# Attention weights times values: two fp32 products per query group made as three split products

## The chip, the cores and the metric

The kernel runs on one core of a Trainium2 chip. Its engines work side by side, each through its own queue of instructions in a fixed order: TensorE (PE; its weight loads are listed as PEld), VectorE (DVE), ScalarE (ACT), GpSimd (POOL) and SyncE (SP, which issues most of the DMAs). They wait for one another through semaphores. The metric is the time of one launch on the device, in microseconds; the median of several runs is compared.

## The reference

One layer of a diffusion backbone for two groups of requests: 256 context tokens (`xp`) and 2048 latent tokens (`xs`), model width 1024. What matters here is the differential attention of the latent tokens, 4 heads, keys and values being 512 cached ones and the 2048 latent ones:

```python
def one_block(qblk):
    s = jnp.einsum('bqhmd,bkhmd->bhmqk', qblk, k).astype(jnp.float32) * scale
    p = jax.nn.softmax(s, axis=-1)
    a = p[:, :, 0] - lam * p[:, :, 1]
    return jnp.einsum('bhqk,bkhe->bqhe', a.astype(v.dtype), v)
```

Around it stand a modulated RMS norm and one input projection before, and a Fourier mixing of other channels, an output projection and a squared-ReLU MLP behind. All inputs are float32.

## The kernel before

**Precision.** A float32 product is mostly made as three products of the type `float32r` (`mm3`, lines 85 to 88): each operand is split into a high part (a rounding copy on ScalarE) and a low part (the original minus the high part, on VectorE), and high·high, high·low and low·high are added up in the same PSUM bank. A few products are made directly in float32 instead, with one matmul call and no low part.

**Stages.** Projections of all tokens, Fourier mixing, attention, output projection, MLP. In the projections `v_out` (lines 343 to 351) copies each tile of values out of PSUM; for the latent tokens it stores it to the DRAM scratch `vs`, and `v_split` stores the high and low parts to `vd`.

**Attention of the latent tokens.** For each of 4 heads, 8 groups of 256 queries, two tiles of 128 (`j`). A group has for each `j` two score maps `m` of 128 x 2560. Operations are methods of `Group`:

- `fill` (line 918): two matmuls of 512 keys into one of five PSUM banks `S`
- `rowmax` (L923) and `comb` (L926): row maxima on VectorE and their combination, once for each `(j, m)`
- `exp` (L942): exponentials on ScalarE from the `S` bank to SBUF, `P0` or `P1`; it needs `comb`, and frees the bank
- `combine` (L946 to L965): denominators on VectorE and POOL, then POOL makes P0 + factor·P1, in two pieces
- `tr` (L974): four transposes of a pair of key blocks `kb`, `kb + 1` into one of **two** PSUM banks `pt`
- `ah` (L980): ScalarE copies that bank to SBUF
- `al` (L985): VectorE subtracts the copy from the bank, the low part
- `mul`: six split products per pair (three for each of two key tiles) into `po`, or, for the pairs named in `FULL = (4, 14)`, two fp32 products (L998) with fp32 values `vf4`, `vf14`, loaded by `load_v` (L878). For these pairs the `ah` copy is fp32 and there is no `al`
- `o1` to `o6`: transposing back, RMS sub-norm and store

The ten pairs of a group are 0, 2, ... 18, so two of them, 4 and 14, go by fp32.

**The order of the work is written out by hand.** Each operation is added to a list with a time (`add`), the list is sorted, and each engine gets its instructions in that order (`tc.manual_schedule()`). The unit of the plan is a step `T`, one for each `(j, m)`, divided into 5 `u`; a group has four steps and the next group follows four steps later. In a step a group's five `fill`s stand at 0.76 to 3.4, its `rowmax`es at 1.26 to 3.9, `comb` at 4.55, and the `exp`s at 0 to 2.64 of the step after. In its steps 6 to 9 the group's pairs are transposed: two in steps 6 and 8, three in steps 7 and 9. In a step of three the transposes stand at 0.9, 2.2 and 3.86, the copies at 3.3, 3.8 and 4.4; the fp32 pair is the first of the three. A step's `mul`s stand at 3.9 of the step after. So the `mul`s of a step of two are on TensorE's queue right behind the third transposes of a step of three, and the `mul`s of a step of three, fp32 ones first, at the end of a step of two. `o1` to `o6` fall into every second step of three. The tile framework adds the waits: `tr` takes a bank `pt` only when everything that reads the tile before in it is done. The plan's times set only the order; they are not waited for.

The last group of the last head takes its transposes' banks from the five `S` and the two `pt` in turn (`bank`, `self.edge`), and some of the first two groups' scores do so too. The prompt's own attention (`Prompt`, one for each head) is laid between the groups, and uses the same `pt` banks.

Of the kernel before, what the change touches and what calls it, by code (L numbers as in the profile page):

```python
# [10 lines left out]
F32 = mybir.dt.float32  # L11
F32R = mybir.dt.float32r
# [6 lines left out]
P = 128  # L19
# [3 lines left out]
NS = 2048  # L23
# [5 lines left out]
LAM_INIT = 0.8 - 0.6 * math.exp(-0.3 * 0)  # L29
GRID_W = 64  # L30
TSTEP, AVS = 5.2, 6
FULL = (4, 14)

PSCALE = 512 / math.sqrt(256 * 128)

# [1 line left out]
def f32(ap):  # L37
    return ap.bitcast(F32)


def body(tc, a, out):
    nc = tc.nc
    ctx = ExitStack()
    with ctx:
# [6 lines left out]
        def scratch(name, shape):  # L51
            return dram.tile(shape, F32, tag=name, name=name)

        fp, fs = scratch("fp", [NP, 512]), scratch("fs", [NS // 2, 512])
        fsum, fdif, frev = (scratch(x, [NS // 2, 512]) for x in ("fsum", "fdif", "frev"))
        vs = scratch("vs", [NS, 512])
        NK = (PAST + NS, NP)
        kd = [scratch(f"kd{s}", [H, 2, P, NK[s]]) for s in range(2)]
        vd = [scratch(f"vd{s}", [H, P, NK[s] // P, 2, P]) for s in range(2)]
# [25 lines left out]
        def mm3(ps, lh, ll, rh, rl, first, last):  # L85
            nc.tensor.matmul(ps, lh, rh, start=first, stop=False)  # L86
            nc.tensor.matmul(ps, lh, rl, start=False, stop=False)  # L87
            nc.tensor.matmul(ps, ll, rh, start=False, stop=last)  # L88
# [119 lines left out]
        with ExitStack() as c1:  # L208
# [6 lines left out]
            def t2(nm):  # L215
                return p1.tile([P, 512], F32, tag="t2", name=nm, bufs=6)
# [127 lines left out]
            def v_out(i):  # L344
                s = 1 if i < 2 else 0
                n = i if s else i - 2
                ps = PJ.pop((i, 2))
                o = t2(f"vo{i}")
                nc.scalar.copy(o, ps)
                nc.sync.dma_start(out[3][n * P:n * P + P] if s else vs[n * P:n * P + P], o)  # L350
                return o

            def v_post(i):
# [55 lines left out]
            with tc.manual_schedule():  # L409
# [30 lines left out]
                with tc.tile_pool(name="p0h", bufs=6, reuse_waits="tile") as halves:  # L440
# [51 lines left out]
                    for k in range(KD):  # L492
                        for g in range(4):
                            w = wraw[2 * k + g // 2][:, g % 2 * 512:g % 2 * 512 + 512]
# [149 lines left out]
        with ExitStack() as c2:  # L644
# [106 lines left out]
            with tc.manual_schedule():  # L751
# [30 lines left out]
                A = [None] * 4  # L782
# [58 lines left out]
        with ExitStack() as c3_:  # L841
# [4 lines left out]
            at = c3_.enter_context(tc.tile_pool(name="a_t", bufs=2, reuse_waits="tile"))  # L846
# [5 lines left out]
            class Head:  # L852
# [16 lines left out]
                def load_v(self):  # L869
                    s, h, ak = self.s, self.h, self.ak  # L870
                    self.V = ak.tile([P, self.nkt, 2, P], F32R, tag=f"V_{s}", name=f"V{self.nm}")
                    nc.sync.dma_start(f32(self.V), vd[s][h])
                    self.vf = {}
                    if not s:
                        for kb in FULL:
                            t = ak.tile([P, 2, P], F32, tag=f"vf{kb}", name=f"vf{kb}{self.nm}")
                            r = (kb - 4) * P
                            nc.sync.dma_start(t, vs[r:r + 2 * P, self.hc].rearrange("(t p) e -> p t e", p=P))  # L878
                            self.vf[kb] = t

            class Group:
                def __init__(self, hd, g):
# [92 lines left out]
                    self.pt[kb] = pt  # L975

                def ah(self, kb):
                    full = kb in self.hd.vf
                    t = at.tile([P, 512], F32 if full else F32R, tag="af" if full else "ah", name=f"ah{self.nm}_{kb}", bufs=2 if full else 4)
                    nc.scalar.copy(t, self.pt[kb])  # L980
                    self.A[kb] = [t]

                def al(self, kb):
                    t = at.tile([P, 512], F32R, tag="al", name=f"al{self.nm}_{kb}", bufs=4)
                    nc.vector.tensor_sub(t, self.pt[kb], f32(self.A[kb][0]))  # L985
                    self.A[kb].append(t)

                def mul(self, kb):
                    if self.po is None:
                        self.po = pS.tile([P, 512], F32, tag="po", name=f"po{self.nm}")  # L990
                    A = self.A.pop(kb)
                    for t in range(2):
                        c = slice(t * 256, t * 256 + 256)
                        first = self.nmul == 0
                        self.nmul += 1
                        last = self.nmul == self.hd.nkt
                        if len(A) == 1:
                            nc.tensor.matmul(self.po[:, 0:256], self.hd.vf[kb][:, t, :], A[0][:, c], start=first, stop=last)  # L998
                        else:
                            mm3(self.po[:, 0:256], self.hd.V[:, kb + t, 0, :], self.hd.V[:, kb + t, 1, :], A[0][:, c], A[1][:, c], first, last)  # L1000

                def o1(self):
                    self.oT = at.tile([P, 256], F32, tag="oT", name=f"oT{self.nm}")
# [81 lines left out]
            def add(t, fn, *args):  # L1085
                ev.append((t, len(ev), fn, args))

            T = TSTEP
            u = T / 5.0
# [11 lines left out]
            for h in range(H):  # L1101
                hd, hp = Head(0, h), Head(1, h)
                base = h * 32 * T
                add(base - 18 * T + 0.7 if h else -3.04 * T, hd.load_k)
                add(base - 14 * T + 0.7 if h else 0.9 * T, hd.load_v)
                add(base - 13 * T + 0.7 if h else 0.91 * T, hp.load_k)
                add(base - 13 * T + 0.71 if h else 0.92 * T, hp.load_v)
                gp, r = Prompt(hp, 0), base + 10 * T
                add(r - 2 * T, gp.qload)
                for j in range(2):  # L1110
                    for t, fn in ((5.25, gp.scores), (5.85, gp.rowmax), (6.33, gp.exp), (8.0, gp.combine)):
                        add(r + t * u, fn, j)
                    r += 2 * T
                for t, fn, *args in ((5.25, gp.tr, 0), (6.33, gp.ah), (6.95, gp.al), (15.25, gp.mul), (16.33, gp.o1),
                                     (25.25, gp.o2), (25.9, gp.o3), (27.32, gp.o4), (28.557, gp.o5), (29.0, gp.o6)):
                    add(r + t * u, fn, *args)
                for g in range(hd.ng):
                    gr = Group(hd, g)
                    add(base - 2 * T + 0.6 * u if base else -3.03 * T, gr.qload)
                    for st in range(4):  # L1120
                        j, m = divmod(st, 2)
                        t0 = base + st * T
                        for b in range(hd.nbk):
                            add(t0 - T + (0.76 + 0.66 * b) * u, gr.fill, j, m, b)
                            add(t0 - T + (1.26 + 0.66 * b) * u, gr.rowmax, j, m, b)
                            add(t0 + 0.66 * b * u, gr.exp, j, m, b)
                        add(t0 - 0.45 * u, gr.comb, j, m)
                        if m:
                            add(t0 + 5.9 * u, gr.combine, j)
                    kbs = list(range(0, hd.nkt, 2))  # L1130
                    for q in range(4):
                        w = base + (AVS + q) * T
                        if q % 2 == 0:
                            order = [kbs.pop(0) for _ in range(2)]
                            tr_t, ah_t, al_t = [0.9, 2.2], [3.3, 3.8], [4.6, 5.2]
                        else:
                            order = [kbs.pop(0) for _ in range(3)]
                            tr_t, ah_t, al_t = [0.9, 2.2, 3.86], [3.3, 3.8, 4.4], [None, 4.6, 5.2]
                        for n, kb in enumerate(order):
                            add(w + tr_t[n] * u, gr.tr, kb)  # L1140
                            add(w + ah_t[n] * u, gr.ah, kb)
                            if al_t[n]:
                                add(w + al_t[n] * u, gr.al, kb)
                            add(w + T + (3.9 + 0.01 * n) * u, gr.mul, kb)
                    w = base + (AVS + 5) * T + 1.0 * u
                    for t, fn in ((0, gr.o1), (0.4, gr.o2), (0.75, gr.o3), (2.32, gr.o4), (3.557, gr.o5), (4.0, gr.o6)):
                        if gr.last and t > 2:
                            LASTO.append(fn)
                        else:
                            add(w + t * u, fn)  # L1150
                    base += 4 * T
# [340 lines left out]
        with c5r, ExitStack() as c5:  # L1492
# [155 lines left out]
            with tc.manual_schedule():  # L1648
                for n, (q, p) in enumerate(ITEMS):
                    b, last = q // NF, q % NF == NF - 1 and q // NF < 2  # L1650
# [71 lines left out]
        with ExitStack() as c6:  # L1722
# [52 lines left out]
            for i in range(7):  # L1775
                for k in range(16):
                    n = i * 16 + k
# [7 lines left out]
            with tc.manual_schedule():  # L1785
                pend, NM, loaded, KS = None, 7 * 24, 4, []
                for i in range(7):
                    for b in range(3):
                        ps = [pp.tile([P, 512], F32, tag="ps", name=f"ps{i}_{b}_{j}", bufs=6) for j in range(3)]
                        for k in range(16):  # L1790
                            n, m = i * 16 + k, (i * 3 + b) * 8 + k // 2
# [18 lines left out]
                            if (i, b) == (6, 2) and 9 <= k < 12:  # L1810

                                j = k - 9
                                u = U3[6 + j]
                                nc.vector.tensor_mul(u, u, g2[0][:, 0:512])
                                nc.vector.tensor_add(u, u, X[j])
                            if i == 0 and b == 1 and k in (2, 6, 10, 14):
                                s, hf = divmod(k // 4, 2)
# [4 lines left out]
                            for j in range(3):  # L1822
                                c = slice(j * P, j * P + P)
# [4 lines left out]
                for j in range(3):  # L1828
                    t = 6 + j
                    c = t6.tile([P, 512], F32, tag="c", name=f"cl{t}", bufs=4)  # L1830
                    nc.vector.tensor_mul(c, ps[j], g2[0][:, 0:512])
                    nc.vector.tensor_sub(c, U3[t], c)
                    r = (t + NTH) * P - NP
# [72 lines left out]
```

## Time and profile before

| | |
|---|---|
| median of 3 runs | 2970.22 us (2969.95 to 2972.25) |
| the profiled execution | 2976.96 us, its span 2975.1 us |
| PE, busy share of the span | 98% |
| DVE | 68% |
| ACT | 53% |
| POOL | 34% |
| mean granted clock of TensorE | 0.993 |

A row of a group reads: line, engine, operation, output tile<-input tiles, shapes, count, then durations. In the timeline a row has start, length, engine, line, operation and, in brackets, how long the engine was idle before it and what ended that. Busy shares overlap: matmuls are pipelined, and a record lasts longer than the time until the next may start. `PEclk` and "granted clock" are the share of its full clock that TensorE was given.

### The profile page before, as it was taken

What the parts mean: (1) busy time and instruction counts of PE and PEld (TensorE: products, weight loads), DVE (VectorE), ACT (ScalarE), POOL (GpSimd) and SP (SyncE); (2) the same over time, 40 slices, a digit from 0 to 9 for tenths busy, and PEclk for the clock granted to TensorE, in tenths of its full rate; (3) what the DMA queues carried; (4) which work ended last, traced back from release to release, by engine and by line L of the source; (5) the groups of instructions that cost most, each with busy time, mean ns of one, the idle gap of its engine ahead of it and who ended that gap; (6) DMA issues with size and microseconds to landing.
All of it is one profiled execution on the core that took longest, in us unless ns stands there. A gap on an engine that the chain in (4) does not pass through costs nothing.

```text
span 2975.1 us, 43755 instructions
## 1 busy us (share of the span) xinstructions
PE 2910.2 (98%) x15417; PEld 2518.0 (85%) x15417; DVE 2016.3 (68%) x3379; ACT 1568.3 (53%) x3540; POOL 1023.9 (34%) x839
## 2 busy tenths in 40 slices
PE   8999999989999999999999999999999999999999
PEld 4888887768888888888889999999999888888887
DVE  6666775678888888875458778777776344344554
ACT  4333322678888888864346556556555322232221
POOL 1111112169898989952222333333332000000000
PEclk9999999989999999999999999999999999999999
DMA  7777878512131211215686677676666454445563
GB/s 274 202 195 198 232 197 250 195 52 84 35 110 37 91 53 34 95 50 157 202 252 213 217 240 225 220 237 214 222 199 229 145 170 163 138 145 173 195 216 107
DMA packets 394414, 495.58 MB, mean 167 GB/s; under 512 B 26403, under 2 KB 307056, under 8 KB 391122
## 3 DMA queue, kind: packets, MB, share of 16 engines
q1 hardware_dynamic: 386560, 477.63, 50.5%
q0 software_dynamic: 2992, 7.28, 0.8%
q10 hardware_dynamic: 4642, 7.88, 0.8%
q8 instruction: 122, 2.00, 0.3%
q14 instruction: 98, 0.80, 0.1%
HBM read 315.20 MB, written 179.57 MB: 166 GB/s over the span
## 4 chain that ended last, share of the span: by engine, by line
PE 84%; ACT 8%; DVE 4%; DMA 2%; issue 1%; POOL 0%; SPq 0%; ACTq 0%; DVEq 0%; POOLq 0%
PE Ss L918 8%; PE ps L86 8%; PE ps L87 8%; PE ps L88 8%; PE pj L86 4%; PE pj L88 4%; PE pj L87 4%; PE pts L974 4%; ACT P1s L942 3%; PE po L88 2%; PE po L86 2%; PE po L87 2%; PE pA L1532 2%; PE pA L1534 2%; PE pA L1533 2%; PE pC L1534 2%
## 5 line engine op out<-in xcount | busy, mean ns | idle before, releaser
L923 DVE TENSOR_REDUCE mxs<-Ss 128x1 f32<-128x512 f32 x640 | 419.4, 687 | 86.8 <-PE Ss L918 77.9
L1227 DVE TENSOR_TENSOR sl<-sr,sh 128x768 fp32r<-128x768 f32 x168 | 161.8, 964 | 339.8 <-ACT sh L1226 339.3
L965 POOL TENSOR_TENSOR P0s<-P0s,P1s 128x1024 f32<-128x1024 f32 x124 | 365.7, 2949 | 10.4
L1226 ACT CAST sh<-sr 128x768 fp32r<-128x768 f32 x168 | 140.2, 835 | 424.9 <-PE ps L87 424.9
L942 ACT ACTIVATE P1s<-Ss,mxs 128x512 f32<-128x512 f32 x320 | 217.2, 694 | 69.3 <-DVE mxs L926 69.3
L1574 POOL TENSOR_TENSOR gs<-g,g 128x384 f32<-128x384 f32 x48 | 70.3, 1464 | 483.7 <-ACT g L1544 376.7
L86 PE MATMUL pj<-wh,hh 128*128 128x512 f32 x576 | 229.8, 399 | 0.7 <-ACT fo L374 0.7
L87 PE MATMUL ps<-tlT,sh 128*128 128x512 f32 x585 | 229.3, 392 | 0.0
L86 PE MATMUL ps<-thT,sh 128*128 128x512 f32 x585 | 229.2, 392 | 0.0
L87 PE MATMUL pj<-wl,hh 128*128 128x512 f32 x576 | 227.7, 395 | 0.7 <-DVE wl L496 0.7
L88 PE MATMUL ps<-thT,sl 128*128 128x512 f32 x585 | 227.7, 389 | 0.0
L88 PE MATMUL pj<-wh,hl 128*128 128x512 f32 x576 | 226.7, 394 | 0.0
L942 ACT ACTIVATE P0s<-Ss,mxs 128x512 f32<-128x512 f32 x320 | 215.8, 696 | 7.8 <-DVE mxs L926 7.7
L918 PE MATMUL Ss<-KS1s,Qs 128*128 128x512 f32 x640 | 199.9, 426 | 13.6 <-ACT P0s L942 11.1
L918 PE MATMUL Ss<-KS0s,Qs 128*128 128x512 f32 x640 | 198.7, 423 | 10.5 <-ACT P1s L942 9.4
L974 PEld LDWEIGHTS pts<-ident,P0s 128*128 128x128 f32 x1280 | 158.0, 141 | 51.7 <-ACT ahs L980 5.7
L974 PE MATMUL pts<-ident,P0s 128*128 128x128 f32 x1280 | 193.0, 274 | 6.3 <-DVE alp L1071 4.1
L1543 ACT ACTIVATE g<-uz 128x384 f32<-128x384 f32 x144 | 75.9, 527 | 207.1 <-DVE uz L1566 180.6
L964 POOL TENSOR_SCALAR P1s<-P1s,tots 128x1024 f32<-128x1024 f32 x124 | 166.7, 1344 | 5.6
L985 DVE TENSOR_TENSOR als<-pts,ahs 128x512 fp32r<-128x512 f32 x256 | 163.9, 681 | 5.3 <-ACT ahs L980 5.3
L86 PE MATMUL ps<-ophT,sh 128*128 128x512 f32 x423 | 165.9, 392 | 1.1 <-DVE uz L1566 1.1
L88 PE MATMUL ps<-ophT,sl 128*128 128x512 f32 x423 | 165.7, 392 | 0.0
(613 smaller groups left out, 8216.1 us busy)
## 6 DMA issues: line engine op xcount, KB each, us to landing
sr<-sd SPq DMA_DIRECT2D x84, 768.0 KB, 4.4
a<-in_w SPq DMA_DIRECT2D x184, 256.0 KB, 3.8
sd<-gs SPq DMA_DIRECT2D x192, 192.0 KB, 1.9
sd<-g SPq DMA_DIRECT2D x144, 192.0 KB, 4.1
wm<-in_w_mod SPq DMA_DIRECT2D x32, 512.0 KB, 5.3
Qs<-qd SPq DMA_DIRECT2D x32, 512.0 KB, 3.7
b<-in_w SPq DMA_DIRECT2D x64, 256.0 KB, 5.2
b<-tsum SPq DMA_DIRECT2D x64, 256.0 KB, 4.6
```

The costliest lines, as they stand in the source:

```text
L86: nc.tensor.matmul(ps, lh, rh, start=first, stop=False)
L87: nc.tensor.matmul(ps, lh, rl, start=False, stop=False)
L88: nc.tensor.matmul(ps, ll, rh, start=False, stop=last)
L918: nc.tensor.matmul(S[:, :w], self.Q[:, x, m, j * P:j * P + P], self.hd.KS[m][:, b * 512:b * 512 + w], start=(x == 0), stop=(x == 1))
L923: nc.vector.tensor_reduce(self.mx[j][:, m, b:b + 1], self.S[j, m, b], axis=AX.X, op=ALU.max)
L942: nc.scalar.activation(dst, S, AF.Exp, bias=self.mx[j][:, m, 6:7], accum_out=self.sm[j][:, m, b:b + 1])
L964: nc.gpsimd.tensor_scalar(p, p, tot[:, 3:4], 0.0, op0=ALU.mult, op1=ALU.add)
L965: nc.gpsimd.tensor_add(d, d, p)
L974: nc.tensor.transpose(pt[:, c:c + P], self.p0[j][:, (kb + t) * P:(kb + t + 1) * P], ident)
L985: nc.vector.tensor_sub(t, self.pt[kb], f32(self.A[kb][0]))
L1226: nc.scalar.copy(hi, src)
L1227: nc.vector.tensor_sub(lo, src, f32(hi))
```

## The change

The two pairs 4 and 14 are treated like the others. Their `ah` copy is `float32r`, they get an `al` subtraction, and `mul` makes six split products of each with the parts of V that are loaded anyway. The fp32 copy of the latent values goes: no scratch `vs`, no stores to it in `v_out`, no `vf` tiles or loads. `ah` and `al` have five buffers each (before four and four, and two for the fp32 copies). In the steps of three the subtractions stand at 4.6, 5.2 and 5.8 of the step (before none, 4.6 and 5.2); transposes and copies keep their places.

```diff
-FULL = (4, 14)
...
-        vs = scratch("vs", [NS, 512])
...
                 nc.scalar.copy(o, ps)
-                nc.sync.dma_start(out[3][n * P:n * P + P] if s else vs[n * P:n * P + P], o)
+                if s:
+                    nc.sync.dma_start(out[3][n * P:n * P + P], o)
                 return o
...
                     nc.sync.dma_start(f32(self.V), vd[s][h])
-                    self.vf = {}
-                    if not s:
-                        for kb in FULL:
-                            t = ak.tile([P, 2, P], F32, tag=f"vf{kb}", name=f"vf{kb}{self.nm}")
-                            r = (kb - 4) * P
-                            nc.sync.dma_start(t, vs[r:r + 2 * P, self.hc].rearrange("(t p) e -> p t e", p=P))
-                            self.vf[kb] = t
...
                 def ah(self, kb):
-                    full = kb in self.hd.vf
-                    t = at.tile([P, 512], F32 if full else F32R, tag="af" if full else "ah", name=f"ah{self.nm}_{kb}", bufs=2 if full else 4)
+                    t = at.tile([P, 512], F32R, tag="ah", name=f"ah{self.nm}_{kb}", bufs=5)
...
                 def al(self, kb):
-                    t = at.tile([P, 512], F32R, tag="al", name=f"al{self.nm}_{kb}", bufs=4)
+                    t = at.tile([P, 512], F32R, tag="al", name=f"al{self.nm}_{kb}", bufs=5)
...
-                        if len(A) == 1:
-                            nc.tensor.matmul(self.po[:, 0:256], self.hd.vf[kb][:, t, :], A[0][:, c], start=first, stop=last)
-                        else:
-                            mm3(self.po[:, 0:256], self.hd.V[:, kb + t, 0, :], self.hd.V[:, kb + t, 1, :], A[0][:, c], A[1][:, c], first, last)
+                        mm3(self.po[:, 0:256], self.hd.V[:, kb + t, 0, :], self.hd.V[:, kb + t, 1, :], A[0][:, c], A[1][:, c], first, last)
...
-                            tr_t, ah_t, al_t = [0.9, 2.2, 3.86], [3.3, 3.8, 4.4], [None, 4.6, 5.2]
+                            tr_t, ah_t, al_t = [0.9, 2.2, 3.86], [3.3, 3.8, 4.4], [4.6, 5.2, 5.8]
                         for n, kb in enumerate(order):
                             add(w + tr_t[n] * u, gr.tr, kb)
                             add(w + ah_t[n] * u, gr.ah, kb)
-                            if al_t[n]:
-                                add(w + al_t[n] * u, gr.al, kb)
+                            add(w + al_t[n] * u, gr.al, kb)
```

## The prediction

> **What bounds the kernel now.** I read the page first, then the windows by stage, then the attention stage's timeline engine by engine.
>
> ```profile
> PE 84%; ACT 8%; DVE 4%; DMA 2%; issue 1%; POOL 0%; SPq 0%; ACTq 0%; DVEq 0%; POOLq 0%
> 150.00:300.00 150.00, 150.00 (x737) 125.06 (x736) 99.47 (x186) 51.16 (x108) 23.87 (x12) 1.00 0.78 200
> 609.00:1326.00 717.00, 698.38 (x4413) 592.95 (x4412) 611.78 (x1199) 618.87 (x1744) 620.58 (x501) 0.99 0.18 63
> L998 PE MATMUL pos<-ahs,vf4s x128: 377/379/382, 624.8 to 1320.1; 128*128 128x256 f32 x128
> L998 PE MATMUL pos<-ahs,vf14s x128: 377/379/382, 635.6 to 1325.0; 128*128 128x256 f32 x128
> L985 DVE TENSOR_TENSOR als<-pts,ahs x256: 675/681/692, 613.5 to 1324.1; 128x512 fp32r<-128x512 f32 x128
> ```
>
> The chain of waits is TensorE's. In the projections (150 to 300 us, where the removed stores are issued) it is never idle. The latent attention with its products fills 609 to 1326 us: 32 groups, 22.4 us each, with PE, DVE, ACT and POOL (the busy columns after the length, PEld second) all between 611 and 698 of 717 us. Four full engines mean that an added wait is not soaked up. Each fp32 product leaves two matmul records (256 records, 128 products, four a group).
>
> A group is four steps; second and fourth ("odd" here) transpose three key-block pairs, the others two. This is one odd step and the even one behind it, on PE.
>
> ```profile
> 902.09 0.62 PE L918 MATMUL Ss<-KS0s,Qs 128*128 128x512 f32 x2
> 904.28 1.17 PE L918 MATMUL Ss<-KS0s,Qs 128*128 128x512 f32 x4
> 905.29 0.60 PE L974 MATMUL pts<-ident,P0s 128*128 128x128 f32 x4
> 905.84 0.28 PE L87 MATMUL pos<-als,Vs 128*128 128x256 f32 x1
> 907.02 0.28 PE L88 MATMUL pos<-ahs,Vs 128*128 128x256 f32 x1
> 907.37 0.73 PE L918 MATMUL Ss<-KS1s,Qs 128*128 128x512 f32 x2
> 910.68 1.02 PE L998 MATMUL pos<-ahs,vf14s 128*128 128x256 f32 x4
> 912.81 0.28 PE L88 MATMUL pos<-ahs,Vs 128*128 128x256 f32 x1
> 912.93 0.63 PE L918 MATMUL Ss<-KS0s,Qs 128*128 128x512 f32 x2
> ```
>
> The odd step takes 907.37 − 902.09 = 5.28 us, the even one 5.56. The third transposes stand at 905.29, and behind them in PE's queue twelve products and the next scores. The other engines then:
>
> ```profile
> 904.46 0.60 ACT L980 COPY ahs<-pts 128x512 f32<-128x512 f32 x1
> 905.12 0.53 PEld L974 LDWEIGHTS pts<-ident,P0s 128*128 128x128 f32 x4
> 905.98 0.59 ACT L980 CAST ahs<-pts 128x512 fp32r<-128x512 f32 x1 [0.43 <-PE pts L974]
> 903.66 2.65 DVE L923 TENSOR_REDUCE mxs<-Ss 128x1 f32<-128x512 f32 x4 [0.21 <-PE Ss L918]
> 906.34 0.16 DVE L926 TENSOR_REDUCE mxs<-mxs 128x1 f32<-128x5 f32 x1
> 906.42 1.28 DVE L985 TENSOR_TENSOR als<-pts,ahs 128x512 fp32r<-128x512 f32 x2
> 908.13 0.69 DVE L923 TENSOR_REDUCE mxs<-Ss 128x1 f32<-128x512 f32 x1 [0.17 <-PE Ss L918]
> 906.53 0.69 ACT L942 ACTIVATE P0s<-Ss,mxs 128x512 f32<-128x512 f32 x1
> 907.37 0.30 PEld L918 LDWEIGHTS Ss<-KS1s,Qs 128*128 128x128 f32 x2 [0.27 <-ACT P0s L942]
> ```
>
> The third transposes load at 905.12, just after the copy of the first pair (904.46 + 0.60) has freed one of the two `pt` banks. That first pair is the fp32 one: copied, never subtracted. DVE's subtractions of the other two begin only at 906.42, behind five row maxima and their combination, and the exponentials' first must follow the third copy (905.98) on ACT; it releases the next step's first scores at 907.37.
>
> **The change part by part.** *Products.* Two fp32 products and twelve split ones take 912.93 − 910.68 = 2.25 us. Ten split intervals from 905.84 to 907.02 are 0.118 us each; eighteen are 2.12. Gain 0.13 us an even step if PE sets its end, nothing if the exponentials do; both lie close, so I take 0.12: 64 × 0.12 = **−8 us** (bounds −8.3 and 0).
>
> *Subtractions.* One more in each odd step, 64 × 0.68 = 44 us of DVE, which has 717 − 612 = 105 us idle in the stage. By itself it is covered by DVE's idle time before the next row maximum; without that cover, see the second rival.
>
> *The new wait.* The first pair is now subtracted too, so its bank is held until that subtraction ends. It is queued on DVE at 4.6 of the step, behind the row maxima and the combination (3.9 and 4.55); the third transposes stay at 3.86 in PE's queue. So PE, which keeps its written order, must wait there. Does such a wait block PE? The trace already has it, once a head, where the prompt's subtraction holds the bank:
>
> ```profile
> 664.91 0.68 DVE L1071 TENSOR_TENSOR alp<-ptp,ahp 128x512 fp32r<-128x512 f32 x1
> 665.71 0.42 PEld L974 LDWEIGHTS pts<-ident,P0s 128*128 128x128 f32 x4 [1.41 <-PE Ss L918]
> PEld pts L974 <- ACT ahs L980: 5.7, 23, 1.9
> PE pts L974 <- DVE alp L1071: 4.1, 4, 1.0
> ```
>
> The transposes load 0.12 us after the subtraction ends (665.59), and nothing behind them passes. So in the step above: first subtraction 906.42 to 907.10, load at 907.22 instead of 905.12, **2.10 us late**. What is late next: transposes, third copy, first exponential (906.53 → 908.63), next scores (907.37 → 909.47), all by 2.10. PE's own twelve products end at 907.14 + 2.10 = 909.24, earlier, so ACT's path sets it. The new third subtraction, at 908.7 behind the third copy, ends before the next row maximum, itself moved to 910.2. The other odd step, four steps of output added:
>
> ```profile
> 915.36 1.17 PE L918 MATMUL Ss<-KS0s,Qs 128*128 128x512 f32 x4
> 916.25 0.48 PEld L974 LDWEIGHTS pts<-ident,P0s 128*128 128x128 f32 x4
> 917.59 1.28 DVE L985 TENSOR_TENSOR als<-pts,ahs 128x512 fp32r<-128x512 f32 x2
> 917.78 0.70 ACT L942 ACTIVATE P0s<-Ss,mxs 128x512 f32<-128x512 f32 x1
> ```
>
> Load at 917.59 + 0.68 + 0.12 = 918.39 instead of 916.25; the third copy then runs 919.2 to 919.8 and the exponential starts 2.02 late. The mean is 2.06. The last group spreads its transposes over seven banks, so 62 of 64 odd steps pay: 62 × 2.06 = **+128 us**. Other odd steps that I read gave 1.83 to 2.18: bounds 113 and 135.
>
> *The clock.* PE's gap in those steps runs from the end of the scores (904.28 + 1.17 = 905.45) to 907.39, and 916.53 to 918.56: about 1.98 us. The trace shows gaps of that kind. Each pair of rows below is a stretch of 3.41 us and the next; after the length stands PE's busy time, third from the end the granted clock.
>
> ```profile
> 574.63:578.04 3.41, 2.04 (x7) 0.89 (x6) 2.93 (x6) 2.68 (x9) 0.00 (x0) 1.00 1.06 354
> 578.04:581.46 3.42, 3.42 (x8) 2.21 (x8) 2.59 (x6) 2.94 (x11) 0.00 (x0) 0.50 0.97 364
> 1298.26:1301.67 3.41, 1.63 (x13) 1.16 (x12) 0.74 (x2) 3.41 (x11) 3.33 (x2) 1.00 0.01 2
> 1301.67:1305.08 3.41, 3.34 (x16) 3.34 (x17) 2.45 (x7) 1.78 (x7) 3.07 (x5) 0.50 0.00 0
> 663.36:666.78 3.42, 2.41 (x16) 1.83 (x14) 2.80 (x5) 3.39 (x13) 3.34 (x2) 1.00 0.00 0
> 666.78:670.19 3.41, 3.34 (x26) 2.87 (x24) 3.17 (x9) 2.63 (x7) 2.01 (x5) 1.00 0.00 0
> 2042.40:2045.80 3.40, 1.99 (x11) 1.83 (x11) 3.16 (x4) 3.37 (x7) 0.00 (x0) 1.00 0.41 130
> 2045.80:2049.20 3.40, 3.40 (x20) 3.18 (x20) 3.40 (x4) 3.01 (x7) 1.35 (x1) 1.00 0.90 263
> ```
>
> Idle 1.37 and 1.78 us in such a stretch were followed by one at half clock, idle 1.01 was not; 1.41 once was not. So the line is near 1.4. A gap of 1.98 at a random phase lies whole in one stretch with chance (3.41 − 1.98) ÷ 3.41 = 0.42, and cut in two, one part is still over 1.4 with 0.58 × 0.59 = 0.34. That is 0.76, some 47 of 62. A half-clock stretch costs at most 3.41 ÷ 2 = 1.71 us of PE; 0.2 to 0.4 us of slack before the next scores takes some of it, so 1.4: 47 × 1.4 = **+65 us**. Bounds: none, and 62 × 1.71 = 106.
> The Trainium skill speaks against this term: in "TensorE: Matmul & The Clock Gate", section "Why this matters for your kernels", only PE-idle gaps over about 3 us between bursts cost the clock. By that the term is nothing; the pair at 574.63 disagrees with it at a gap of 1.37, and I go by the row.
>
> *Transfers.* Sixteen stores of v and eight fp32 loads go. Nothing in the projections waits on them (PE 150 of 150 us), and the loads are ahead of need: 0, bounds −2 and 0. The extra `ah`/`al` buffers equal the five pairs alive at once: 0.
>
> Sum: −8 + 128 + 65 = +185 us. The profiled execution took 2976.96 us (span 2975.1), 6.7 above the median of the runs, 2970.22; its span gives 3162, but the comparison is between medians: **3155 us**.
>
> **The rivals.** (1) *The wait comes, the clock holds*: 2970 + 120 = **3090 us**. For it, the stretch at 2042.40; against it, those at 574.63 and 1298.26. This is also what the skill's rule gives. (2) *No wait, DVE is the bound*: were the bank released by the copy alone, three subtractions in a row would end at 908.30, the denominators at 908.57, and the row maximum would start 0.45 late, of which 0.21 is idle time before the next: about 0.2 to the exponential. The even step, with 0.13 taken off PE, then grows by some 0.07: 64 × 0.07 = +4, **2975 us**. (3) *Faster*: the same release, and DVE's idle time hides the subtraction wholly: 2970 − 8 = **2962 us**. It decides at one point, whether the third transposes still load at 905.1. Against both: the subtraction reads `pt`, and the row at 665.71 waits for just such a reader.
>
> **How the numbers follow.** Forecast 0.67, rival (1) 0.25, (2) 0.03, (3) 0.05. The range takes in (1): low 2970 + 113 − 8 = 3075 with the clock held; high 2970 + 135 + 106 = 3211. A measurement of this kernel can tell 0.2%, 6 us, from no change: faster 0.05, same 0.03, slower 0.92.
>
> **What would show it.** The waits: third transposes held by `als` some 62 times, near 2 us each. Subtractions 320 instead of 256, no L998-like records. A group near 28.2 us ((717 + 185) ÷ 32). Granted clock over the stage near 0.91 (47 × 1.71 us lost of 902), against 0.99. Wrong would be: those transposes held by the copy only (no wait at all), or waits of 2 us with a clock still at 0.99.

## The result and the profile after

The changed kernel takes 3121.94 us (median of 4 runs, 3119.85 to 3124.09) against 2971.23 us in the same comparison: a ratio of 1.0501, 95% interval 1.0486 to 1.0516. It is slower by 151 us; 3155 us had been forecast. Its profiled execution took 3119.85 us, span 3118.0.

The page of the changed kernel, its chain of waits and two of its groups (idle time before the group and its releaser at the end):

```profile
PE 85%; DVE 8%; DMA 3%; issue 2%; ACT 1%; POOL 0%; SPq 0%; ACTq 0%; DVEq 0%; POOLq 0%
L966 PE MATMUL pts<-ident,P0s 128*128 128x128 f32 x1280 | 201.9, 283 | 117.9 <-DVE als L976 113.6
L976 DVE TENSOR_TENSOR als<-pts,ahs 128x512 fp32r<-128x512 f32 x320 | 207.7, 683 | 58.0 <-ACT ahs L971 57.8
```

The transposes' idle time was 6.3 us on the page of before; now it is 117.9, and 113.6 of it end with a subtraction. DVE has taken ACT's place as the chain's second engine. The waits of the attention stage (who waited for whom: us in total, times, longest):

```profile
PE pts L966 <- DVE als L976: 113.6, 62, 3.4
```

Sixty-two waits, the number forecast, 1.83 us each. By windows, the attention stage and two pairs of stretches of 3.41 us within it (length, then PE's busy time; granted clock third from the end). 3.41 us is how long each spell at half clock in this stage lasts:

```profile
609.00:1469.00 860.00, 737.23 (x4551) 619.75 (x4549) 656.02 (x1264) 621.99 (x1748) 623.14 (x502) 0.95 0.14 52
933.64:937.05 3.41, 1.74 (x10) 1.09 (x8) 3.30 (x7) 1.85 (x6) 2.71 (x1) 1.00 0.02 5
937.05:940.46 3.41, 3.27 (x24) 2.92 (x24) 1.98 (x5) 2.57 (x8) 0.70 (x3) 1.00 0.00 0
947.30:950.70 3.40, 1.54 (x11) 0.98 (x9) 3.27 (x7) 1.91 (x8) 2.88 (x3) 0.99 0.00 0
950.70:954.11 3.41, 3.41 (x16) 3.16 (x15) 0.93 (x3) 3.14 (x9) 1.66 (x5) 0.51 0.53 174
```

The stage grew from 717 to 860 us, which is the whole difference of the spans (143 us). DVE's work grew by 44 us, as the added subtractions had been counted, POOL's by 3. PE now has 123 idle us in it (19 before). A stretch with 1.67 us idle was followed by full clock, one with 1.86 by half clock.

One odd step, the even step behind it and the wait of the next odd one on PE; then the DVE rows of the first:

```profile
931.91 0.73 PE L910 MATMUL Ss<-KS0s,Qs 128*128 128x512 f32 x2
934.20 1.18 PE L910 MATMUL Ss<-KS0s,Qs 128*128 128x512 f32 x4
937.17 0.63 PE L966 MATMUL pts<-ident,P0s 128*128 128x128 f32 x4 [1.79 <-DVE als L976]
938.91 0.28 PE L86 MATMUL pos<-ahs,Vs 128*128 128x256 f32 x1
939.21 0.73 PE L910 MATMUL Ss<-KS1s,Qs 128*128 128x512 f32 x2
944.65 0.73 PE L910 MATMUL Ss<-KS0s,Qs 128*128 128x512 f32 x2
950.23 0.70 PE L966 MATMUL pts<-ident,P0s 128*128 128x128 f32 x4 [1.86 <-DVE als L976]
```

```profile
936.27 0.16 DVE L918 TENSOR_REDUCE mxs<-mxs 128x1 f32<-128x5 f32 x1
936.34 1.28 DVE L976 TENSOR_TENSOR als<-pts,ahs 128x512 fp32r<-128x512 f32 x2
938.51 0.69 DVE L976 TENSOR_TENSOR als<-pts,ahs 128x512 fp32r<-128x512 f32 x1 [0.89 <-ACT ahs L971]
```

The rows run as predicted, in order: maxima, combination, first subtraction to 937.02, third transposes at 937.17, twelve products, next scores. The odd step takes 7.30 us in place of 5.28, the even one 5.44 in place of 5.56.

### The profile page after: what moved, and what is told of

Its sections match the earlier page's. It is cut to its first block, busy times and chain, and to the rows that moved or that the text cites. A ratio compares the mean times of both kernels' runs of the same rounds, so it can differ in the third digit from the quotient of the medians.

```text
span 3118.0 us, 44143 instructions
## 1 busy us (share of the span) xinstructions
PE 2947.1 (95%) x15545; PEld 2543.2 (82%) x15545; DVE 2060.7 (66%) x3443; ACT 1569.5 (50%) x3540; POOL 1023.4 (33%) x839
## 3 DMA queue, kind: packets, MB, share of 16 engines
q8 instruction: 123, 2.02, 0.3%
## 4 chain that ended last, share of the span: by engine, by line
PE 85%; DVE 8%; DMA 3%; issue 2%; ACT 1%; POOL 0%; SPq 0%; ACTq 0%; DVEq 0%; POOLq 0%
PE Ss L910 9%; PE ps L84 7%; PE ps L85 7%; PE ps L86 7%; PE pts L966 5%; PE pj L86 3%; PE pj L85 3%; PE pj L84 3%; DVE mxs L915 3%; PE pos L86 2%; PE pos L85 2%; PE pos L84 2%; PE po L86 2%; PE po L84 2%; PE po L85 2%; PE pA L1519 2%
## 5 line engine op out<-in xcount | busy, mean ns | idle before, releaser
L966 PE MATMUL pts<-ident,P0s 128*128 128x128 f32 x1280 | 201.9, 283 | 117.9 <-DVE als L976 113.6
L971 ACT CAST ahs<-pts 128x512 fp32r<-128x512 f32 x320 | 182.5, 602 | 158.7 <-PE pts L966 158.6
L976 DVE TENSOR_TENSOR als<-pts,ahs 128x512 fp32r<-128x512 f32 x320 | 207.7, 683 | 58.0 <-ACT ahs L971 57.8
L910 PE MATMUL Ss<-KS1s,Qs 128*128 128x512 f32 x640 | 208.3, 440 | 4.4 <-ACT P0s L934 4.1
L84 PE MATMUL pos<-ahs,Vs 128*128 128x256 f32 x640 | 193.3, 302 | 0.0
L86 PE MATMUL pos<-ahs,Vs 128*128 128x256 f32 x640 | 188.6, 295 | 0.0
L85 PE MATMUL pos<-als,Vs 128*128 128x256 f32 x640 | 188.1, 294 | 0.0
```

Source lines behind the costliest of these rows:

```text
L910: nc.tensor.matmul(S[:, :w], self.Q[:, x, m, j * P:j * P + P], self.hd.KS[m][:, b * 512:b * 512 + w], start=(x == 0), stop=(x == 1))
L966: nc.tensor.transpose(pt[:, c:c + P], self.p0[j][:, (kb + t) * P:(kb + t + 1) * P], ident)
```

## The experiments

Times are medians. The kernel before took 2973.2 us beside the first four, 2975.4 beside the next four and 2974.6 beside the last. Differences between experiments of different groups are taken between their ratios.

**The wait taken away, the products kept.** Pairs 4 and 14 get their six products without the subtraction:

```diff
-                            add(w + al_t[n] * u, gr.al, kb)
+                            if kb not in (4, 14):
+                                add(w + al_t[n] * u, gr.al, kb)
...
-                        mm3(self.po[:, 0:256], self.hd.V[:, kb + t, 0, :], self.hd.V[:, kb + t, 1, :], A[0][:, c], A[1][:, c], first, last)
+                        mm3(self.po[:, 0:256], self.hd.V[:, kb + t, 0, :], self.hd.V[:, kb + t, 1, :], A[0][:, c], A[-1][:, c], first, last)
```

> The changed kernel without the new subtraction: pairs 4 and 14 still get six split products each, but with the high part of the weights in place of the low part, so their low part is left out of the result. Theory (the held bank is the cost): nothing waits for the third transposes' bank, and only the products' gain of 0.12 us an even step is left: 2962 us, between 2960 and 2972. Rival (the six products, the buffers or the missing fp32 copy cost the time): it stays above 3050 us.

Measured: 2977.82 us, ratio 1.0015 (1.0005 to 1.0024). The loss is gone, so neither the six products nor the buffers nor the missing fp32 copy make it. But the gain of 8 us did not come either. PE's rows of an odd step, an even one and the other odd one show why:

```profile
901.71 0.73 PE L910 MATMUL Ss<-KS0s,Qs 128*128 128x512 f32 x2
907.08 0.73 PE L910 MATMUL Ss<-KS1s,Qs 128*128 128x512 f32 x2
912.52 0.73 PE L910 MATMUL Ss<-KS0s,Qs 128*128 128x512 f32 x2
918.32 0.73 PE L910 MATMUL Ss<-KS1s,Qs 128*128 128x512 f32 x2 [0.27 <-ACT P0s L934]
```

The even step is 5.44 us, 0.12 shorter as forecast; the first odd one is 5.37, 0.09 longer. In the kernel before, the odd step's first pair of scores took 0.62 us (row at 902.09), its weights being loaded behind the last products; now that pair, too, follows an exponential directly and takes 0.73.

**The wait alone.** The kernel before with an idle subtraction of its fp32 pairs:

```diff
-                            tr_t, ah_t, al_t = [0.9, 2.2, 3.86], [3.3, 3.8, 4.4], [None, 4.6, 5.2]
+                            tr_t, ah_t, al_t = [0.9, 2.2, 3.86], [3.3, 3.8, 4.4], [4.6, 5.2, 5.8]
...
                     nc.vector.tensor_sub(t, self.pt[kb], f32(self.A[kb][0]))
-                    self.A[kb].append(t)
+                    if kb not in self.hd.vf:
+                        self.A[kb].append(t)
```

> The kernel before with its fp32 products, and a subtraction of the pairs 4 and 14 whose result nothing reads, at the changed kernel's places (4.6, 5.2, 5.8). Theory: all of the loss without the products' gain, 3122 + 8 = 3130 us, between 3115 and 3145, with some 62 waits of the third transposes for als. Rival (the products are the cost): below 2990 us.

Measured: 3119.76 us, ratio 1.0499 (1.0482 to 1.0517), with the same waits:

```profile
PE pts L974 <- DVE als L985: 112.8, 62, 3.3
```

One more subtraction that reads the bank, with the fp32 products left as they were, makes the whole loss.

**The clock.** Two products of a zero tile in PE's wait, right ahead of the third transposes:

```diff
+                def warm(self):
+                    first = self.po is None
+                    if first:
+                        self.po = pS.tile([P, 512], F32, tag="po", name=f"po{self.nm}")
+                    self.warmed = True
+                    for i in range(2):
+                        nc.tensor.matmul(self.po[:, 0:256], zt, self.hd.KS[0][:, 0:256], start=first and i == 0, stop=False)
...
+                            add(w + 3.8 * u, gr.warm)
```

> The changed kernel with two products of a zero tile (nothing is added to the result) ahead of each third transposes, inside PE's wait: its gap falls from 1.80 and 1.88 us to some 1.6, the wait's end does not move. Theory (a stretch of 3.41 us with 1.84 us or more of idle PE is followed by one at half clock, and each costs about 1.5 us): no half-clock stretches in the groups, 23 x 1.5 = 33 us less, 3089 us, between 3080 and 3096, granted clock of the stage 0.99 in place of 0.94. Rival (those stretches come from something else, or their cost is hidden): 3118 to 3126 us.

Measured: 3085.19 us, ratio 1.0382 (1.0366 to 1.0397). Of the loss, 1.0501 − 1.0382 = 1.2%, 35 us, was the clock, and work that computes nothing took it away. The changed kernel has 25 spells at half clock in the attention stage, this run two, near 616 and 1412 us; the kernel before has two as well, near 616 and 1302. The attention stage of this run, and its two odd steps on PE:

```profile
609.00:1437.00 828.00, 722.82 (x4679) 612.53 (x4677) 656.07 (x1264) 619.67 (x1749) 622.93 (x502) 0.99 0.15 54
```

```profile
921.56 0.73 PE L913 MATMUL Ss<-KS0s,Qs 128*128 128x512 f32 x2
924.85 0.39 PE L988 MATMUL pos<-KS0s,zt 128*128 128x256 f32 x2
926.82 0.63 PE L969 MATMUL pts<-ident,P0s 128*128 128x128 f32 x4 [1.57 <-DVE als L979]
928.85 0.73 PE L913 MATMUL Ss<-KS1s,Qs 128*128 128x512 f32 x2
934.28 0.73 PE L913 MATMUL Ss<-KS0s,Qs 128*128 128x512 f32 x2
941.77 0.73 PE L913 MATMUL Ss<-KS1s,Qs 128*128 128x512 f32 x2
```

Then one zero product instead of two (`range(1)`):

> As the run with two zero products, with one: the gap of the third transposes falls to about 1.7 and 1.76 us. Theory (the line lies at 1.84 us of idle PE in a stretch, as the changed kernel's stretches show): no half-clock stretches in the groups, the same 3085 us, between 3080 and 3092. Rival (the line lies lower, near 1.4 to 1.7, as the prediction had it): some half-clock stretches stay, 3100 to 3122 us.

Measured: 3091.14 us, ratio 1.0384 (1.0368 to 1.0399). The profiled execution has the same two spells at half clock as with two products, so there a tenth of a microsecond of work in the gap was enough. It was the shortest of the four, though (3082.62 us at a mean clock of 0.994); the others took 3091 to 3094 us at 0.990 to 0.991, so some of the clock's loss is probably left in them.

**What is behind the wait.** Three runs move the two queues' contents apart. First the products ahead of the third transposes:

```diff
-                            add(w + T + (3.9 + 0.01 * n) * u, gr.mul, kb)
+                            add(w + T + (3.9 + 0.01 * n - (0.1 if q % 2 == 0 else 0)) * u, gr.mul, kb)
```

> The changed kernel with the twelve products of a two-pair step put ahead of the third transposes on PE's queue. Theory (the third copy stands before the next step's first exponential on ACT, and that sets the next scores): the wait at the transposes shrinks by the products' 1.42 us to about 0.4 us, but the same time comes back as a wait of the next scores for ACT; gain at most 0.2 us in 62 steps, 3110 to 3124 us. Rival (what is queued behind the transposes on PE sets it): 62 x 1.42 = 88 us less, 3034 us.

Measured: 3116.54 us, ratio 1.0483 (1.0468 to 1.0499). PE's rows of an odd step:

```profile
931.90 0.63 PE L966 MATMUL pts<-ident,P0s 128*128 128x128 f32 x4 [0.39 <-DVE als L976]
933.94 0.73 PE L910 MATMUL Ss<-KS1s,Qs 128*128 128x512 f32 x2 [1.41 <-DVE als L976]
```

The wait moved by one instruction: 0.39 us at the transposes, 1.41 at the next scores. (The profile puts the second on the subtraction; the weight load of those scores waits, by its own row, for ACT's exponential.) Then the other move alone, the third copy and subtraction behind the next step's first exponentials:

```diff
-                            tr_t, ah_t, al_t = [0.9, 2.2, 3.86], [3.3, 3.8, 4.4], [4.6, 5.2, 5.8]
+                            tr_t, ah_t, al_t = [0.9, 2.2, 3.86], [3.3, 3.8, 6.3], [4.6, 5.2, 6.5]
```

> The changed kernel with the third pair's copy and subtraction moved behind the next step's first two exponentials (copy 4.4 to 6.3, subtraction 5.8 to 6.5); the products stay behind the third transposes on PE. Theory (two queues hold the next scores back, each nearly as long: ACT's by the third copy, PE's by the twelve products): freeing ACT alone gains at most 0.2 us a step, 3105 to 3125 us. Rival (ACT's queue alone is the cost): about 62 x 1.7 = 105 us less, 3017 us.

Measured: 3120.21 us, ratio 1.0488 (1.0473 to 1.0504): no gain clear of the noise. Now both:

> The changed kernel with both moves: products ahead of the third transposes, third copy and subtraction behind the next step's first two exponentials. Theory: now nothing that the next scores need stands behind the held bank. PE still ends its third transposes about 0.25 us later than before, and the moved subtraction puts the next row maxima back by about 0.3 us: 2978 + 62 x 0.55 = 3012 us, between 2990 and 3035, no half-clock stretches in the groups. Rival (the wait's cost can't be moved off, the four full engines give it back elsewhere): above 3080 us.

Measured: 3045.02 us, ratio 1.0233 (1.0218 to 1.0249). Each move alone gained at most 5 us, both together 80 (by the ratios), so the two queues do hold the step side by side. Of the 80, 35 are the clock's: between 630 and 1360 us this run was granted 1.00. Against the run with zero products, which has no such loss either, the moves gained 1.0382 − 1.0233, 44 us, or 0.7 us a wait. And 33 us of the forecast gain are missing. ACT's waits in this run name a third hold:

```profile
ACT P0s L934 <- PE pts L966: 41.3, 18, 2.5
```

```profile
913.91 0.69 ACT L934 ACTIVATE P0s<-Ss,mxs 128x512 f32<-128x512 f32 x1 [2.23 <-PE pts L966]
925.44 0.69 ACT L934 ACTIVATE P0s<-Ss,mxs 128x512 f32<-128x512 f32 x1 [0.21 <-DVE mxs L918]
```

The list names 18 such waits, and 12 more of the same exponential for the denominators on DVE (26.2 us). In one odd step of each group the third transposes are the group's last, and the last reader of a `P0` buffer; with five of them, the first exponential of the next tile needs just that one. In the other odd step it starts 0.21 us after its row maxima. With a sixth buffer, for which `ah` gives up one and `al` two of their five:

```diff
-            ap = c3_.enter_context(tc.tile_pool(name="a_p", bufs=5, reuse_waits="tile"))
+            ap = c3_.enter_context(tc.tile_pool(name="a_p", bufs=6, reuse_waits="tile"))
...
-                    t = at.tile([P, 512], F32R, tag="ah", name=f"ah{self.nm}_{kb}", bufs=5)
+                    t = at.tile([P, 512], F32R, tag="ah", name=f"ah{self.nm}_{kb}", bufs=4)
...
-                    t = at.tile([P, 512], F32R, tag="al", name=f"al{self.nm}_{kb}", bufs=5)
+                    t = at.tile([P, 512], F32R, tag="al", name=f"al{self.nm}_{kb}", bufs=3)
```

> As the run with both moves, with a sixth buffer for P0 (room made by one buffer of ah and two of al fewer). Theory (in every second three-pair step the first exponential of P0 also needs the buffer that the third transposes read last, so it waits for them directly): that exponential starts with its row maxima again, 31 x 1.2 = 37 us less, 3008 us, between 2998 and 3022. Rival (what the moves left is something else): 3035 to 3050 us.

Measured: 3011.18 us, ratio 1.0124 (1.0107 to 1.0141): about 33 us less, and both kinds of wait are gone from ACT's list, so the buffer was this hold. 37 us of the loss remain. Most of it stands where it began:

```profile
PE pts L966 <- DVE als L976: 28.4, 62, 4.0
```

DVE does the same 320 subtractions here as in the changed kernel, so its 44 us of added work cost by themselves 37 us at most; no run has them without the held bank.

**What is ahead of it.** The first subtraction before the step's last row maximum (`al_t` [3.5, 5.2, 5.8]):

> The changed kernel with the first pair's subtraction ahead of the step's last row maximum on VectorE (4.6 to 3.5). Theory (the wait is the row maximum and its combination in front of the subtraction): the bank comes free 0.78 us earlier, the third transposes are some 1.0 us late instead of 1.8, and with a gap of 0.9 us there are no half-clock stretches: 2978 + 62 x 1.0 = 3040 us, between 3020 and 3055. Rival (the delayed row maximum costs what the earlier bank gains): 3085 us or more.

Measured: 3037.54 us, ratio 1.0211 (1.0194 to 1.0228). The subtraction now starts before the last row maximum and the combination, and PE's gap is 1.00 us in place of 1.79:

```profile
905.56 0.68 DVE L976 TENSOR_TENSOR als<-pts,ahs 128x512 fp32r<-128x512 f32 x1
906.39 0.63 PE L966 MATMUL pts<-ident,P0s 128*128 128x128 f32 x4 [1.00 <-DVE als L976]
```

Of the 86 us gained, 35 are again the clock's (1.00 between 630 and 1350 us); the other 51 are 0.82 us a wait.

No version with six products for these pairs beat the kernel before. This move, the two others and the sixth buffer were not tried all together.

## Why the prediction was right, and where its sizes were off

The measured time lies inside the range, and the likeliest case is the one that came: the wait, and with it the clock. Against the forecast of +185 us stand 151 between the medians, and 148 in the terms below, which go by the ratios of the runs, on 2972 us:

| Term | forecast | measured | from |
|---|---|---|---|
| products | −8 | +4 | 1.0015, the wait taken away |
| the new wait | +128 | +109 | 1.0382 − 1.0015 |
| the clock | +65 | +35 | 1.0501 − 1.0382 |

*Products.* The 0.12 us an even step was right, and shown by its row; that it is left at the end was not. The bound of nothing, for the case that the exponentials set the end, is what happened: the next odd step gave 0.09 back in a weight load that the products had covered. The remaining +4 us, outside the stated bounds of −8.3 and 0, do not appear in the profiled executions (spans 2974.8 and 2975.1) and stay open.

*The wait.* Mechanism, place and count were right: 62 waits, ended by the subtraction, 2.02 us more in the odd step shown (7.30 − 5.28; forecast 2.10). Mis-sized was the handover. The step was to begin 0.29 us after the subtraction's end (0.12 to the weight load, 0.17 to the first transpose); the rows show 937.17 − 937.02 = 0.15. Against the run without the wait the two odd steps are 1.92 and 1.69 us longer (7.29 − 5.37 and 7.49 − 5.80, rows of the two runs above); over all 62 it is 109 ÷ 62 = 1.76, in place of 2.06, just under the lower bound of 1.83. The handover is 0.14 us of this difference of 0.30. In the first odd step another 0.09 is that the step without the wait had become longer (5.37 in place of 5.28), which is counted under the products. The rest was not traced. That ACT's third copy, not PE's products, would set the step was right by only about 0.1 us: moving the products gained 5 us of the 88 that they fill, and the intervals of the two runs overlap.

*The clock.* That gaps of this kind cost clock was right; the line near 1.4 us, read from the few stretches quoted there, was wrong for the groups, and with it the 47 stretches. Why 1.37 us of idle time was enough at 574.63 stays open, and so does the stretch at 1298.26 with 1.78. Worked out for each stretch of 3.41 us of the changed kernel between 609 and 1446 us from PE's records: none with less than 1.84 us idle was followed by one at half clock, and 19 of them lie at 1.79 to 1.81; each of the 25 with 1.84 or more was. The two odd steps' gaps, 1.79 and 1.86 us in the rows at 937.17 and 950.23, fall on the two sides of that line, so mostly one step of a group pays: 23 spells more than before or with zero products, 35 ÷ 23 = 1.5 us each, where 1.4 was estimated. The price was right, the count of 47 twice too high.
The Trainium skill ("TensorE: Matmul & The Clock Gate", section "Why this matters for your kernels") names gaps over about 3 us. Here 1.86 us within one stretch were enough; by its rule the kernel would have been at the 3085 us of the run with zero products.

*What would show it.* 62 waits and 320 subtractions came as listed; a group is 860 ÷ 32 = 26.9 us where 28.2 was named, and the stage's clock 0.95 where 0.91 was, both by the clock's and the wait's sizes.

*Transfers.* That the removed stores and loads are worth nothing agrees with the run without the subtraction, which has none of them either and is not faster.

The rivals without a wait fall with the 62 waits; the one with the wait and a held clock falls with the granted clock of 0.95, though by its size, 3090 us, it is as near as the forecast: 32 us below the measured time, where 3155 is 33 above. The time alone would not have told them apart; the two zero products made that rival true, at 3085. And the forecast's total is nearer than its terms: the wait and the clock were 49 us too high, and the products, 12 too low, hide a part of that.

## What to carry to other kernels

Before giving a buffer one more reader, look up where that reader stands in its engine's queue: here 0.68 us of work, for which DVE had idle time, kept PE waiting for a PSUM bank 1.8 us, 62 times, because it was queued behind the row maxima. When a wait stands in front of two queues, freeing one shows nothing; move both, then look for the next holder of the same release. And a gap on PE can have a second price, the clock: here gaps of 1.86 us in stretches of 3.41 cost 35 us, which even useless matmuls bought back.

## What was not expected of the hardware

In the changed kernel's trace the line of the clock is sharp: 0.07 us of gap, 1.79 against 1.86, decides on a stretch of 3.41 us at half clock. But it is not the same line in every run. These are two stretches, each with the next one, from the run with the products first and from the one with the copy later:

```profile
971.27:974.69 3.42, 1.64 (x11) 1.15 (x10) 2.37 (x7) 1.81 (x5) 1.55 (x4) 1.00 0.14 38
974.69:978.10 3.41, 3.41 (x15) 2.78 (x12) 1.86 (x3) 2.60 (x9) 3.15 (x4) 0.50 0.45 159
974.67:978.08 3.41, 1.53 (x10) 0.98 (x8) 3.29 (x8) 3.16 (x12) 1.35 (x2) 1.00 0.01 2
978.08:981.49 3.41, 3.41 (x25) 3.20 (x26) 1.55 (x5) 3.40 (x10) 3.05 (x7) 1.00 0.39 120
```

In the first, 1.78 us idle were followed by half clock; in the second, 1.88 were not. So idle time by PE's records is not all that counts, and what else does stays open.

The group's length settles by the clock's stretches. The spells at half clock of the changed kernel come in runs of about six, 27.3 us apart, which is eight stretches, while a group without any takes mostly 25.7 us from one `oT` copy to the next (run with zero products), and one with such a spell mostly 27.1. A group that pays one is nearly as long as eight stretches, so the next one's gap falls in the same place of its stretch and pays as well.
